# Attention in a hybrid encoder layer: the value product in two pieces instead of three, and the softmax sums added on GpSimd and VectorE

## The chip, the core and the metric

The kernel runs on one core of one Trainium2 chip. The metric is the device time of one execution in microseconds (us). The engines are TensorE (PE in the profile, PEld for its weight loads), VectorE (DVE), ScalarE (ACT), GpSimd (POOL) and the queue engine SyncE (SP).

## What is computed

One encoder layer over 2048 + 256 tokens of width 1024, in fp32: a joint input projection, eight mLSTM heads and eight attention heads side by side, an output projection with residual, and a convolutional feed-forward part. The change touches only the attention, whose reference is

```python
def block(qi):
    s = jnp.einsum('bqhgd,bkhd->bhgqk', qi, k).astype(jnp.float32) * scale
    p = jax.nn.softmax(s, axis=-1)
    return jnp.einsum('bhgqk,bkhd->bqhgd', p.astype(v.dtype), v)
```

with 64 columns a head, eight query heads on two key/value groups, and every query seeing all 2048 (or 256) keys of its sequence.

## The kernel before

To keep fp32 accuracy on TensorE, the kernel splits an operand in a rounded high part (type fp32r) and a low part, the rest, and multiplies high x high, high x low and low x high.

Attention (`attention`, lines 458 to 673) works on **head blocks**: 512 queries against all keys of their sequence. There are 36: four for the short sequence, with two key tiles of 128 keys, and 32 with sixteen. A block is walked in **steps** of two key tiles (eight steps, or one), 260 steps in all. One step is:

- `scores` (L577): four products of 512 columns (L583, L584) fill a score tile `ps` of two PSUM banks; ScalarE takes the exponential into `pe` (L587, 128 x 1024) and copies its high part into `x[:, 0]` (L588); VectorE subtracts for the low part `x[:, 1]` (L589).
- `values` (L592), some steps later: per key tile three products add into one PSUM bank `pv`. The stationary operand `vv` holds the high part of the values in columns 0 to 63 and ones in columns 64 to 127, so that rows 64 to 127 of `pv` gather the softmax sums; `vl` holds the low part of the values. L600 is `vv` x high weights, L601 `vl` x high weights, L602 `vv` x low weights.
- `maxstep` (L548): for the next block, two products (L560) and a maximum on VectorE (L562).

At a block's end `fin1` copies both halves of `pv` to SBUF with four ScalarE copies (L612); `fin2`, a step later, takes reciprocals of the sums (L617), multiplies (L618), and GpSimd's queue stores the result to `mix_d` (L624).

The score tiles, the maxima's tiles (`px`) and two small ones share a ring of two (tag "sc"); `pv` is one bank with one buffer. `PEB`, `XB` and `PLAG` are the buffers of `pe`, of `x`, and the number of steps by which `values` runs behind `scores`.

While attention runs, the other half of the program runs between its instructions: until about 1400 us the mLSTM heads (projection products L720, L730, L748; masks loaded by GpSimd's queue at L824 and cut by GpSimd at L828; GpSimd products `kw` at L793 and inverse roots at L97 and L98; VectorE work at L848 to L879), then the output projection (L1001). `run_both` (L1574) interleaves the two generators by weights; a scheduler then gives every engine its fixed order, which the engine follows instruction by instruction.

## Time and profile before

| what | before |
|---|---|
| time, median of 3 runs | 3317.97 us (3317.39 to 3322.92) |
| span of the profiled execution | 3315.5 us |
| busy: PE / weight loads / VectorE / ScalarE / GpSimd | 98% / 91% / 73% / 60% / 16% of the span |
| granted TensorE clock, mean | 0.992 |
| attention's steps | from 224 to about 1752 us |

The profile is of one execution, whose span (first to last instruction) is 3315.5 us. A group row gives line, engine, operation, output and inputs, shapes, count, then busy time and mean ns of one, then the idle time of the engine just before and what ended it. Rows of the timeline give start and length in us. Products overlap on PE, so that the length of one (about 0.40 us at 512 columns) is more than the distance between two.

### The profile page before, as it was taken

How to read it: one execution, taken by the hardware profiler on the slowest of the kernel's cores; microseconds unless marked ns; L12 is line 12 of the kernel's file. 1: busy time of each engine (PE TensorE's matmuls, PEld its weight loads, DVE VectorE, ACT ScalarE, POOL GpSimd, SP SyncE). 2: the span in 40 equal slices, each digit the busy share in tenths (PEclk: the TensorE clock that was granted, in tenths of full speed). 3: DMA queues.
4: the chain of work that ended last, by engine and by line, in shares of the span. 5: the costliest groups of instructions: out<-in, count | busy, mean ns of one | idle time of the engine just before them, and what ended most of it. 6: DMA issues, size and time to landing. Idle time of an engine off the chain costs nothing.

```text
span 3315.5 us, 53149 instructions
## 1 busy us (share of the span) xinstructions
PE 3240.5 (98%) x19488; PEld 3018.0 (91%) x19488; DVE 2429.5 (73%) x3759; ACT 1993.5 (60%) x3738; POOL 522.1 (16%) x917
## 2 busy tenths in 40 slices
PE   8989999999999999999999999999999999999998
PEld 7878888888888888788889999999999999999998
DVE  7755676676657768866666899998888889666654
ACT  5646666666675776655454555665676667454543
POOL 4561042223224323200000000000000000020101
PEclk9999999999999999999999999999999999999999
DMA  9973333343346444423227666767676567968663
GB/s 353 316 213 101 112 103 113 98 125 109 99 139 189 123 147 127 139 96 106 76 93 266 220 222 213 248 229 271 202 254 240 194 224 239 320 216 276 216 226 134
DMA packets 359117, 612.31 MB, mean 185 GB/s; under 512 B 31029, under 2 KB 215271, under 8 KB 358855
## 3 DMA queue, kind: packets, MB, share of 16 engines
q1 hardware_dynamic: 329431, 563.14, 50.5%
q0 software_dynamic: 11856, 33.96, 3.8%
q10 hardware_dynamic: 17568, 11.80, 1.1%
q8 instruction: 154, 2.52, 0.3%
q14 instruction: 108, 0.88, 0.1%
HBM read 444.85 MB, written 163.93 MB: 184 GB/s over the span
## 4 chain that ended last, share of the span: by engine, by line
PE 83%; issue 5%; DMA 4%; ACT 3%; DVE 3%; POOL 2%; SPq 1%; POOLq 0%; ACTq 0%; DVEq 0%
PE pa L1164 17%; PE pc L1164 8%; PE pf L1428 7%; PE po L1001 6%; PE pb L1164 4%; PE mj L720 4%; PE pj L238 4%; PE mv L730 4%; PE ph L1428 3%; PE ps L583 3%; PE pv L602 3%; PE pv L600 3%; PE ps L584 3%; PE pv L601 3%; PE px L560 3%
## 5 line engine op out<-in xcount | busy, mean ns | idle before, releaser
L589 DVE TENSOR_TENSOR xx<-pe,xx 128x1024 fp32r<-128x1024 f32 x260 | 319.0, 1227 | 171.4 <-ACT xx L588 169.9
L587 ACT ACTIVATE pe<-ps 128x1024 f32<-128x1024 f32 x260 | 266.1, 1024 | 231.8 <-PE ps L584 215.0
L562 DVE TENSOR_REDUCE mx<-px 128x1 f32<-128x1024 f32 x256 | 310.5, 1218 | 100.6 <-PE px L560 100.0
L588 ACT ACTIVATE xx<-pe 128x1024 fp32r<-128x1024 f32 x260 | 275.1, 1058 | 5.2 <-PE pv L602 0.2
L1381 POOL TENSOR_TENSOR sq<-sq,sq 128x384 f32<-128x384 f32 x38 | 48.5, 1277 | 1382.7 <-ACT sq L1377 1302.2
L1001 PEld LDWEIGHTS po<-cmx,wo 128*128 128x128 f32 x1728 | 229.9, 189 | 19.5 <-DVE cx L1008 1.1
L1001 PE MATMUL po<-cmx,wo 128*128 128x256 f32 x1728 | 238.7, 283 | 1.4 <-DVE cx L1008 1.0
L1168 ACT ACTIVATE u<-pa 128x386 f32<-128x386 f32 (+2 forms) x264 | 128.9, 489 | 173.9 <-PE pa L1164 168.7
L600 PE MATMUL pv<-xx,vv 128*128 128x512 f32 x520 | 212.4, 408 | 10.5 <-ACT rs L612 6.0
L583 PE MATMUL ps<-qq,kk 128*128 128x512 f32 x520 | 213.8, 411 | 8.2 <-ACT pe L587 3.9
L602 PE MATMUL pv<-xx,vv 128*128 128x512 f32 x520 | 211.0, 406 | 3.5 <-DVE xx L589 3.4
L584 PE MATMUL ps<-qm,kl 65*128 65x512 f32 x520 | 208.9, 402 | 0.0
L601 PE MATMUL pv<-xx,vl 128*64 128x512 f32 x520 | 207.3, 399 | 0.0
L720 PEld LDWEIGHTS mj<-mn,wm 128*128 128x128 f32 x1296 | 178.3, 193 | 18.3 <-ACT og L736 4.5
L720 PE MATMUL mj<-mn,wm 128*128 128x256 f32 x1296 | 189.6, 288 | 2.8 <-ACT og L736 2.8
L730 PE MATMUL mv<-wm,mn 128*128 128x256 f32 x1296 | 189.9, 286 | 1.3 <-ACT qb L726 1.3
L730 PEld LDWEIGHTS mv<-wm,mn 128*128 128x128 f32 x1296 | 176.1, 190 | 15.2 <-ACT qb L726 2.3
L238 PE MATMUL pj<-w_a,n1T 128*128 128x512 f32 (+1 forms) x864 | 167.8, 353 | 11.0 <-ACT w_a L105 7.1
L560 PE MATMUL px<-kk,qq 128*128 128x512 f32 x512 | 167.2, 408 | 2.4 <-ACT pe L587 2.4
L238 PEld LDWEIGHTS pj<-w_a,n1T 128*128 128x128 f32 x864 | 141.3, 192 | 30.6 <-ACT w_a L105 7.1
L1164 PE MATMUL pc<-nt,wb 128*128 128x386 f32 (+2 forms) x792 | 148.0, 341 | 0.0
L831 ACT ACTIVATE dm<-dm,tm 128x128 f32<-128x128 f32 x288 | 94.8, 392 | 86.0 <-POOL dm L828 85.7
(337 smaller groups left out, 8106.0 us busy)
## 6 DMA issues: line engine op xcount, KB each, us to landing
mn<-n_d SPq DMA_DIRECT2D x216, 256.0 KB, 3.1
ru<-w_up SPq DMA_DIRECT2D x88, 512.0 KB, 5.1
rs<-wsu_d SPq DMA_DIRECT2D x88, 512.0 KB, 5.7
act_d<-ts SPq DMA_DIRECT2D x33, 768.0 KB, 6.4
nt<-act_d SPq DMA_DIRECT2D x60, 384.0 KB, 5.2
re_t<-wsd_d SPq DMA_DIRECT2D x45, 512.0 KB, 5.4
wsu_d<-tw SPq DMA_DIRECT2D x44, 512.0 KB, 4.2
act_d<-ya SPq DMA_DIRECT2D x99, 192.0 KB, 2.1
```

Source lines behind the costliest of these rows:

```text
L238: nc.tensor.matmul(pjs[t][:, c0:c1], nTs[tiles[t]][:, c, a, :], ws[c][:, b, c0:c1], start=(c == 0 and k == 0), stop=(c == NCC - 1 and k == 2))
L562: nc.vector.tensor_reduce(s.mx[:, t0, z0:z0 + 1], ps, AX.X, ALU.max)
L583: nc.tensor.matmul(o, kk[:, kc:kc + P], s.qq, start=True, stop=False)
L584: nc.tensor.matmul(o, kl1[:, kc:kc + P], s.qm, start=False, stop=True)
L589: nc.vector.tensor_tensor(x[:, 1], pe, f32(x[:, 0]), ALU.subtract)
L600: nc.tensor.matmul(s.pv, vv[:, kt % 4, :], x1, start=kt == 0, stop=False)
L602: nc.tensor.matmul(s.pv, vv[:, kt % 4, :], x2, start=False, stop=kt == s.nk - 1)
L720: nc.tensor.matmul(pj[:, o].rearrange("p (n t) -> p n t", t=P), s.w[c][:, a, o * P:(o + 1) * P], nT[c][:, :, h, :], start=(c + o + k == 0) ...
L730: nc.tensor.matmul(pv[:, o], nT[c][:, o, a, :], s.w[c][:, h, 256:512], start=(c + o + k == 0), stop=(c == NCC - 1 and k == 2 and o == 1))
L1001: nc.tensor.matmul(po[:, o], wo[c][z // 2][:, a, n], mx[c][:, h, :], start=c + o + k == 0, stop=c == NCC - 1 and o == 1 and k == 2)
L1164: s.nc.tensor.matmul(p, w[:, aa, c, :], ops[k][:, c, bb, 0:s.n], start=c == 0 and i == 0 and not add, stop=c == NCC // 2 - 1 and i == 2, s ...
L1428: nc.tensor.matmul(ps[c], w[:, aa, c, :], t[:, gi - g0, bb, 0:H], start=gi == 0 and m == 0 and not more, stop=gi == NG - 1 and m == 2, ski ...
```

## The change

The value operand `vv` now holds the high part in columns 0 to 63 and the low part in columns 64 to 127, with no ones. Per key tile there are two products: `vv` x high weights (128 rows of `pv`: high and low part of the values) and the high part x low weights (64 rows). At a block's end the two halves of `pv` are added.

The sums are kept apart: from a block's second step on, the exponentials `pe` of the step before are added into this step's `pe`, columns 0 to 511 by GpSimd and 512 to 1023 by VectorE, once the subtraction has read it. After the last step GpSimd adds the two halves (`asum`), the sum is split in high and low part (`fin2`), two products with a tile of ones spread it over all rows (`fin3`), and reciprocal, multiplication and store follow (`fin4`). The three are taken one step after another. The buffers change: `pe` 3, `x` 3, lag 2.

```diff
-PEB = 2
-XB = 4
-PLAG = 3
+PEB = 3
+XB = 3
+PLAG = 2
...
-            vv = sp.tile([P, m, P], F32R, tag="vv" + s, name=f"vv{grp}_{s}", bufs=1)
-            vl = sp.tile([P, m, HD], F32R, tag="vl" + s, name=f"vl{grp}_{s}", bufs=1)
+            vv = sp.tile([P, m, 2, HD], F32R, tag="vv" + s, name=f"vv{grp}_{s}", bufs=1)
...
-            nc.gpsimd.memset(f32(vv[:, :, HD:P]), 1.0)
...
-            for a, t in ((0, vv[:, :, 0:HD]), (1, vl)):
-                nc.gpsimd.dma_start(f32(t), g.v_d[grp, :, k0 + t0:k0 + t0 + m, a])
+            nc.gpsimd.dma_start(f32(vv), g.v_d[grp, :, k0 + t0:k0 + t0 + m])
...
         nc.vector.tensor_tensor(x[:, 1], pe, f32(x[:, 0]), ALU.subtract)
+        if kp:
+            for z, eng in ((0, nc.gpsimd), (1, nc.vector)):
+                c = slice(512 * z, 512 * z + 512)
+                eng.tensor_tensor(pe[:, c], s.acc[:, c], pe[:, c], ALU.add)
+        s.acc = pe
+        if kp == s.nk // 2 - 1:
+            s.acc = sp.tile([P, 512], F32, tag="asum", name="asum" + s.nm, bufs=1)
+            nc.gpsimd.tensor_tensor(s.acc, pe[:, 0:512], pe[:, 512:1024], ALU.add)
...
-            nc.tensor.matmul(s.pv, vv[:, kt % 4, :], x1, start=kt == 0, stop=False)
-            nc.tensor.matmul(s.pv[0:HD], vl[:, kt % 4, :], x1, start=False, stop=False)
-            nc.tensor.matmul(s.pv, vv[:, kt % 4, :], x2, start=False, stop=kt == s.nk - 1)
+            for a in (0, 1) if z == 0 else (1, 0):
+                if a:
+                    nc.tensor.matmul(s.pv[0:HD], vv[:, kt % 4, 0], x2, start=False, stop=False)
+                else:
+                    nc.tensor.matmul(s.pv, vv[:, kt % 4].rearrange("p a d -> p (a d)"), x1, start=kt == 0,
+                                     stop=kt == s.nk - 1)
...
-            for r, o in ((0, s.o1), (HD, s.rs)):
-                nc.scalar.activation(o[HD * z:HD * z + HD], s.pv[r:r + HD, 256 * z:256 * z + 256], AF.Copy)
+            r, c = slice(HD * z, HD * z + HD), slice(256 * z, 256 * z + 256)
+            nc.scalar.activation(o2[r], s.pv[HD:P, c], AF.Copy)
+            nc.vector.tensor_tensor(s.o1[r], s.pv[0:HD, c], o2[r], ALU.add)
+
+    def fin2(s):
+
+        s.ah = sp.tile([P, 2, 512], F32R, tag="ah", name="ah" + s.nm, bufs=1)
+        nc.scalar.activation(s.ah[:, 0], s.acc, AF.Copy)
+        nc.vector.tensor_tensor(s.ah[:, 1], s.acc, f32(s.ah[:, 0]), ALU.subtract)
+
+    def fin3(s):
+
+        ps = pp.tile([P, 1024], F32, tag="sc", name="pa" + s.nm)
+        for a in range(2):
+            nc.tensor.matmul(ps[:, 0:512], g.onesr, s.ah[:, a], start=a == 0, stop=a == 1)
...
+            nc.scalar.activation(s.rs[r], ps[r, c], AF.Copy)
```

Since the scheduler sets the order, three places show what moved. In these rows a line number belongs to its own kernel (L600 to L602 before are L607 and L609 after, L589 is L586, L562 is L559, and L590 is the new addition); "waits" names the engine waited for; x3 counts equal rows.

TensorE before, in a block of head 4 while an mLSTM projection runs; `pv` is the value bank, `xx` the weights of a step, `ps` the scores:

```order
L602 MATMUL pv_4_5855<-xx_4_2_5825,vv_16_4_2556 128x512 [waits DVE_49]
L600 MATMUL pv_4_5855<-xx_4_2_5825,vv_16_4_2556 128x512
L601 MATMUL pv_4_5855<-xx_4_2_5825,vl_16_4_2557 64x512
L602 MATMUL pv_4_5855<-xx_4_2_5825,vv_16_4_2556 128x512
L583 MATMUL ps_4_4_6050<-qq_4_5303,kk_16_8_2570 128x512 [waits Activation_49]
L584 MATMUL ps_4_4_6050<-qm_4_5305,kl_16_8_2571 128x512
L583 MATMUL ps_4_4_6050<-qq_4_5303,kk_16_8_2570 128x512
L584 MATMUL ps_4_4_6050<-qm_4_5305,kl_16_8_2571 128x512
L600 MATMUL pv_4_5855<-xx_4_3_5851,vv_16_4_2556 128x512 [waits Activation_49]
L601 MATMUL pv_4_5855<-xx_4_3_5851,vl_16_4_2557 64x512
```

TensorE after, at the same step of the same block (`mj`, `mN`: mLSTM):

```order
L580 MATMUL ps_4_4_6108<-qq_4_5350,kk_16_8_2561 128x512 [waits DVE_49]
L581 MATMUL ps_4_4_6108<-qm_4_5352,kl_16_8_2562 128x512
L580 MATMUL ps_4_4_6108<-qq_4_5350,kk_16_8_2561 128x512
L581 MATMUL ps_4_4_6108<-qm_4_5352,kl_16_8_2562 128x512
L609 MATMUL pv_4_5891<-xx_4_3_5909,vv_16_4_2551 128x512 [waits Activation_49]
L745 MATMUL mj_6_7560<-mn_6_4_7548,wm_4_4882 128x256 [waits DMAHW7_49]
L745 MATMUL mj_6_7560<-mn_6_4_7548,wm_4_4882 128x256 x3
L888 MATMUL mN_16_7894<-va_8_2400,dm_16_7530 128x65 [waits DMASW7_49,PE_49,Activation_49]
L888 MATMUL mN_16_7894<-va_8_2400,dm_16_7530 128x65 x3
L607 MATMUL pv_4_5891<-xx_4_3_5909,vv_16_4_2551 64x512 [waits DVE_49]
L607 MATMUL pv_4_5891<-xx_4_3_5909,vv_16_4_2551 64x512
L609 MATMUL pv_4_5891<-xx_4_3_5909,vv_16_4_2551 128x512
```

The step's values are four products in place of six; those of the low weights (L607, the ones that wait for VectorE's subtraction) stand in the middle, with mLSTM products ahead of them.

VectorE before, a little earlier in the same block (`mx` is a maximum, `hh` and `s` belong to mLSTM):

```order
L562 TENSOR_REDUCE mx_4_5722<-px_4_0_1_5841 128x1 [waits PE_49]
L589 TENSOR_TENSOR xx_4_2_5825<-pe_4_2_5824,xx_4_2_5825 128x1024 [waits Activation_49]
L877 TENSOR_TENSOR hh_12_7041<-hh_12_7041,mr_12_7046 128x128 [waits DVE_49,Activation_49,Pool_49]
L879 SCALAR_TENSOR_TENSOR hh_12_7041<-ogr_12_6669,hh_12_7041 128x128 [waits DMASW3_49,DVE_49]
L562 TENSOR_REDUCE mx_4_5722<-px_4_1_1_5862 128x1 [waits PE_49]
L589 TENSOR_TENSOR xx_4_3_5851<-pe_4_3_5850,xx_4_3_5851 128x1024 [waits Activation_49]
L562 TENSOR_REDUCE mx_4_5722<-px_4_2_1_6066 128x1 [waits PE_49]
L589 TENSOR_TENSOR xx_4_4_6056<-pe_4_4_6055,xx_4_4_6056 128x1024 [waits Activation_49]
```

VectorE after, at the same steps; `pe` is the exponential, in which the sum is carried on, and `C` the mLSTM state:

```order
L559 TENSOR_REDUCE mx_4_5778<-px_4_0_1_5896 128x1 [waits PE_49]
L879 TENSOR_TENSOR s_16_7784<-mI_16_7781,tm 128x260 [waits PE_49]
L902 TENSOR_TENSOR hh_15_7767<-hh_15_7767,mr_15_7772 128x128 [waits DVE_49,Activation_49,Pool_49]
L586 TENSOR_TENSOR xx_4_2_5885<-pe_4_2_5884,xx_4_2_5885 128x1024 [waits Activation_49]
L904 SCALAR_TENSOR_TENSOR hh_15_7767<-ogr_14_7153,hh_15_7767 128x128 [waits DVE_49]
L559 TENSOR_REDUCE mx_4_5778<-px_4_1_1_5919 128x1 [waits PE_49]
L842 SCALAR_TENSOR_TENSOR C_9_4927<-C_8_4926,dec,C_9_4927 128x65 [waits Activation_49]
L590 TENSOR_TENSOR pe_4_2_5884<-pe_4_1_5854,pe_4_2_5884 128x512 [waits DVE_49]
L842 SCALAR_TENSOR_TENSOR C_10_4928<-C_9_4927,dec,C_10_4928 128x65 [waits DVE_49,Activation_49]
L586 TENSOR_TENSOR xx_4_3_5909<-pe_4_3_5908,xx_4_3_5909 128x1024 [waits Activation_49]
L590 TENSOR_TENSOR pe_4_3_5908<-pe_4_2_5884,pe_4_3_5908 128x512 [waits DVE_49]
```

Behind each subtraction (L586) stands an addition of half a tile (L590), once with a state update between, once right behind it; it waits for VectorE's own subtraction, and everything below it waits with it.

GpSimd before, in the same block (`dm` is a mask, `mr` an inverse root, `kw` an mLSTM product, `o` a block's result):

```order
L97 TENSOR_SCALAR mr_11_6914<-mms_11_6911 128x2 [waits Activation_49]
L98 TENSOR_TENSOR mr_11_6914<-mr_11_6914,mhalf 128x2 [waits Pool_49]
L836 DMA ogr_16_7457<-og_d 128x256 [waits DMAHW0_49,DMASW3_49,DVE_49]
L737 MEMSET va_4_4910 128x4
L793 TENSOR_TENSOR kw_6_6802<-mkt_3_6800,tm 128x256 [waits PE_49]
L793 TENSOR_TENSOR kw_7_6804<-mkt_3_6800,tm 128x256 [waits PE_49]
L624 DMA mix_d<-o_4_5835 64x256 [waits DVE_49,Activation_49]
L624 DMA mix_d<-o_4_5835 64x256 [waits DMASW5_49,Activation_49]
L824 DMA dm_15_7313<-nm_d 128x512 [waits DMASW6_49,PE_49]
L828 AFFINE_SELECT dm_15_7313<-dm_15_7313 128x256 [waits DMASW6_49]
L828 AFFINE_SELECT dm_15_7313<-dm_15_7313 128x256
```

GpSimd after, at the end of the block before and the start of this one; `asum` is the folded sum:

```order
L590 TENSOR_TENSOR pe_4_7_5754<-pe_4_6_5738,pe_4_7_5754 128x512 [waits DVE_49,Pool_49]
L594 TENSOR_TENSOR asum_4_5761<-pe_4_7_5754 128x512 [waits DVE_49,Pool_49]
L853 AFFINE_SELECT dm_17_7786<-dm_17_7786 128x256 [waits DMASW1_49]
L853 AFFINE_SELECT dm_17_7786<-dm_17_7786 128x256
L750 MEMSET qb_7_4958 64x2x128 [waits PE_49]
L750 MEMSET qb_7_4958 64x2x128 [waits Pool_49]
L97 TENSOR_SCALAR mr_14_7516<-mms_14_7513 128x2 [waits Activation_49,Pool_49]
L98 TENSOR_TENSOR mr_14_7516<-mr_14_7516,mhalf 128x2 [waits Pool_49]
L590 TENSOR_TENSOR pe_4_1_5854<-pe_4_0_5784,pe_4_1_5854 128x512 [waits DVE_49]
L849 DMA dm_0_8687<-nm_d 128x512 [waits PE_49]
L853 AFFINE_SELECT dm_0_8687<-dm_0_8687 128x256 [waits DMASW2_49]
```

The additions and the fold stand in one line with the masks' loads, cuts and inverse roots. An addition waits for VectorE (the subtraction that reads the same tile), and masks and roots wait behind it; the cut behind a load waits for that load, and the additions behind it.

More of the change, by code (lines that the diff above doesn't have):

```diff
@@ L493, in load_kv @@
             nc.gpsimd.memset(f32(kl1[64:65, :]), 1.0)
-            for a, t in ((0, vv[:, :, 0:HD]), (1, vl)):
-                nc.gpsimd.dma_start(f32(t), g.v_d[grp, :, k0 + t0:k0 + t0 + m, a])
-            parts.append((kk, kl1, vv, vl))
+            nc.gpsimd.dma_start(f32(vv), g.v_d[grp, :, k0 + t0:k0 + t0 + m])
+            parts.append((kk, kl1, vv))
     class HB:
@@ L643, in drain @@
             fin1(b)
-            fins.append(b)
+            fins.extend((f, b) for f in (fin2, fin3, fin4))
     for n in range(len(hbs)):
@@ L652, in attention @@
             pend.append((cur, *scores(cur, kp)))
-            ready = bool(fins)
+            ready = fins.pop(0) if fins else None
             if len(pend) > PLAG:
@@ L661, in attention @@
             if ready:
-                fin2(fins.pop(0))
+                ready[0](ready[1])
             yield 2.3
@@ L671, in attention @@
         yield 1
-    for b in fins:
-        fin2(b)
+    for f, b in fins:
+        f(b)
 def mlstm(g, tc, s1, sp, sw, sn, pj_, pm):
@@ L1522, in body @@
             sk = pool(s2, "b_k", bufs=1)
+            g.onesr = sk.tile([P, P], F32R, name="onesr")
+            nc.gpsimd.memset(f32(g.onesr), 1.0)
             sa = pool(s2, "b_s", bufs=2)
```

11 lines of the change are left out of this document (7 added, 4 removed).

## The prediction

> **What bounds the kernel now.** I read the head of the profile's page first, then the busy times of three stretches, then the groups of instructions, then the timeline. The page gives the span of the one profiled execution and the busy time of every engine; the stretches are from the first softmax step to the last mLSTM tile, from there to the last softmax step, and all that follows (columns: start and end, length, busy time and count of PE, PEld, DVE, ACT, POOL, granted clock, DMA share, GB/s).
>
> ```profile
> span 3315.5 us, 53149 instructions
> PE 3240.5 (98%) x19488; PEld 3018.0 (91%) x19488; DVE 2429.5 (73%) x3759; ACT 1993.5 (60%) x3738; POOL 522.1 (16%) x917
> ```
>
> ```profile
> 224.00:1400.00 1176.00, 1150.98 (x7264) 1001.94 (x7263) 807.82 (x1516) 767.48 (x1754) 331.48 (x652) 1.00 0.41 125
> 1400.00:1752.00 352.00, 344.88 (x2141) 298.69 (x2142) 235.51 (x329) 193.68 (x272) 14.69 (x23) 1.00 0.29 95
> 1752.00:3315.00 1563.00, 1538.27 (x8884) 1535.65 (x8882) 1221.22 (x1536) 908.38 (x1479) 58.64 (x50) 0.99 0.68 234
> ```
>
> The change touches only attention, so only the first two stretches, 1528 us together. PE is busy in 1495.9 of them (98%), VectorE in 1043.3 (68%), ScalarE in 961.2 (63%), GpSimd in 346.2. The groups say what a softmax step (one pair of key tiles) costs; there are 260 steps in 36 head blocks, 256 of them in 32 blocks of eight.
>
> ```profile
> L589 DVE TENSOR_TENSOR xx<-pe,xx 128x1024 fp32r<-128x1024 f32 x260 | 319.0, 1227 | 171.4 <-ACT xx L588 169.9
> L562 DVE TENSOR_REDUCE mx<-px 128x1 f32<-128x1024 f32 x256 | 310.5, 1218 | 100.6 <-PE px L560 100.0
> L588 ACT ACTIVATE xx<-pe 128x1024 fp32r<-128x1024 f32 x260 | 275.1, 1058 | 5.2 <-PE pv L602 0.2
> L587 ACT ACTIVATE pe<-ps 128x1024 f32<-128x1024 f32 x260 | 266.1, 1024 | 231.8 <-PE ps L584 215.0 <-DVE xx L589 5.3 <-DVE mx L562 3.2
> L600 PE MATMUL pv<-xx,vv 128*128 128x512 f32 x520 | 212.4, 408 | 10.5 <-ACT rs L612 6.0 <-ACT xx L588 4.1
> L602 PE MATMUL pv<-xx,vv 128*128 128x512 f32 x520 | 211.0, 406 | 3.5 <-DVE xx L589 3.4
> L601 PE MATMUL pv<-xx,vl 128*64 128x512 f32 x520 | 207.3, 399 | 0.0
> ```
>
> VectorE waits for ScalarE (171.4 us), ScalarE for PE (231.8 us), PE for next to nobody: PE sets the pace. But 0.40 us is a product's own length, not its price, since products overlap. The timeline of PE gives the price.
>
> ```profile
> 1500.02 0.40 PE L602 MATMUL pv<-xx,vv 128*128 128x512 f32 x1
> 1500.26 0.39 PE L600 MATMUL pv<-xx,vv 128*128 128x512 f32 x1
> 1500.49 0.39 PE L601 MATMUL pv<-xx,vl 128*64 128x512 f32 x1
> 1500.72 0.39 PE L602 MATMUL pv<-xx,vv 128*128 128x512 f32 x1
> 1500.95 0.28 PE L1001 MATMUL po<-cmx,wo 128*128 128x256 f32 x1
> ```
>
> Four products start within 0.93 us: 0.2325 us each, and the one with a 64-column stationary operand costs no less.
>
> **The products taken away.** A key tile has two value products in place of three: 520 fewer. Each head block gets two products with ones: 72 more. Net 448 x 0.2325 = 104.2 us of PE, 0.40 us a step. If PE went on setting the pace, the span would fall by that. The Trainium skill ("Perfetto Trace Analysis", section "Identifying the Most-Contended Engine") says to judge TensorE by the busy share of its weight loads rather than of its matmuls. That share is 85% in the first stretch and 98% in the last, so by the rule the gain would be cut to about 0.87 of it, an estimate of 91 us. The trace speaks against it here: a 0.19 us load under a 0.2325 us product cannot show more than 82%, and the five rows above have no gap. I keep 104.2.
>
> **The additions.** The row sums now come from VectorE (columns 512 to 1023 of the weights) and GpSimd (0 to 511), in 224 of the 260 steps (not in a block's first). Each block also folds its halves on GpSimd, splits the sum on VectorE and ScalarE, and adds the two halves of its result on VectorE. The nearest rows of those shapes, then of GpSimd (lowest, median and highest ns):
>
> ```profile
> L1015 DVE TENSOR_TENSOR cacc<-cacc,csq 128x512 f32<-128x512 f32 x26 | 17.9, 688 | 9.4 <-ACT csq L1011 9.3
> L864 DVE TENSOR_TENSOR s<-mN,s 128x260 f32<-128x260 f32 x72 | 30.1, 419 | 15.5 <-PE mN L863 15.3
> L612 ACT ACTIVATE rs<-pv 64x256 f32<-64x256 f32 x72 | 27.3, 380 | 1.6
> L539 ACT ACTIVATE qq<-pq 128x512 fp32r<-128x512 f32 x36 | 21.4, 594 | 5.5 <-PE pq L536 5.2
> ```
>
> ```profile
> L793 POOL TENSOR_TENSOR kw<-mkt,tm x72: 605/617/1682, 236.5 to 1220.7; 128x256 f32<-128x256 f32 x72
> L1381 POOL TENSOR_TENSOR sq<-sq,sq x38: 992/1133/1881, 2845.3 to 3281.9; 128x384 f32<-128x384 f32 x38
> L589 DVE TENSOR_TENSOR xx<-pe,xx x260: 1160/1224/1570, 224.0 to 1751.5; 128x1024 fp32r<-128x1024 f32 x130
> ```
>
> VectorE: 224 x 0.688 = 154.1, 36 x 0.688 = 24.8, 72 x 0.419 = 30.2, together 209.1 us or 0.804 us a step. ScalarE: 144 copies of 0.38 go; 144 of 0.38 and 36 of 0.594 come: +21 us on an engine with 37% to spare, which costs nothing as long as the exponential isn't late. GpSimd: from 256 to 384 columns the undisturbed time rises by 0.387 us, and by proportion from 384 it is 1.32 us; I take 1.35 us for 512 columns, between 1.32 and 1.38. 260 of them are 351 us: GpSimd doubles from 346 to 697 us. Fewer loads and fills of key and value tiles are a few us of GpSimd, off the path.
>
> Costed at nothing: the value products follow two steps behind the scores instead of three, with three weight tiles instead of four. Two steps are some 11 us, and the chain of exponential, copy and subtraction is 1.02 + 1.06 + 1.23 = 3.3 us, so 7 us of queueing are covered; beyond that each late subtraction stops PE. The sums' products take one turn more of the two score banks in each block, held for 2 x 0.2325 and two copies of 0.38, 1.2 us; the projection products of mLSTM and of phase C hide it, and it would cost 36 x 1.2 = 44 us if they didn't.
>
> **Who shares what.** The highest times above are no accident: a subtraction of 1.57 us and a kw of 1.68 us each overlapped the other engine.
>
> ```profile
> 304.88 1.23 DVE L589 TENSOR_TENSOR xx<-pe,xx 128x1024 fp32r<-128x1024 f32 x1 [2.66 <-ACT xx L588]
> 480.46 1.57 DVE L589 TENSOR_TENSOR xx<-pe,xx 128x1024 fp32r<-128x1024 f32 x1 [0.78 <-ACT xx L588]
> ```
>
> ```profile
> 304.90 1.68 POOL L793 TENSOR_TENSOR kw<-mkt,tm 128x256 f32<-128x256 f32 x1 [18.13 <-PE mu L806]
> 480.33 0.62 POOL L793 TENSOR_TENSOR kw<-mkt,tm 128x256 f32<-128x256 f32 x1 [1.46 <-PE mu L806]
> ```
>
> At 304.9 kw began 0.02 us behind the subtraction and took 1.06 us longer than its median: it waited it out. At 480.3 kw was first, and the subtraction took 0.35 us longer. So a VectorE operation with two inputs from SBUF and a GpSimd operation exclude one another, nearly from end to end. A GpSimd addition can therefore hold VectorE up by anything from 0 to 1.1 us (1.35 less the 0.25 that these pairs leave open). Both halves become ready when the subtraction ends. In 57 of 224 cases VectorE's half stands right behind the subtraction and goes first; else one to four others stand between, mostly reductions from PSUM or one-input work that need not wait. I take b = 0.4 us of delay a step, about a third of the 1.1.
>
> **The sum.** VectorE isn't evenly loaded. The busy times of the densest windows, then the subtractions in the same windows (which count steps), and a later window for what VectorE can reach:
>
> ```profile
> 400.00:500.00 100.00, 98.11 (x617) 85.32 (x617) 80.81 (x167) 69.38 (x164) 35.98 (x70) 1.00 0.34 102
> 700.00:800.00 100.00, 99.58 (x646) 88.37 (x645) 77.56 (x173) 66.59 (x163) 35.90 (x75) 1.00 0.39 116
> 1100.00:1400.00 300.00, 290.85 (x1741) 245.98 (x1742) 234.92 (x481) 205.39 (x477) 86.79 (x163) 0.99 0.42 129
> 2000.00:2100.00 100.00, 100.00 (x568) 99.96 (x567) 95.04 (x121) 59.61 (x93) 0.00 (x0) 1.00 0.59 207
> ```
>
> ```profile
> 400.00:500.00 100.00, 21.11 (x17) 1.00 0.34 102
> 700.00:800.00 100.00, 19.52 (x16) 1.00 0.39 116
> 1100.00:1400.00 300.00, 64.97 (x53) 0.99 0.42 129
> ```
>
> Dense part: 500 us, 86 steps, VectorE 393.3. It becomes 393.3 + 86 x (0.804 + 0.4) = 496.8; at the 95% that the window at 2000 shows, this needs 523.0 us: **+23.0**, since PE (500 - 86 x 0.40) no longer binds. The other 1028 us, 174 steps: VectorE 650.0 + 174 x 1.204 = 859.5, or 904.8 at 95%; PE 1028 - 69.8 = 958.2 still binds: **-69.8**. Handing over the one pv bank at a block's end: before, four copies of 0.38 on ScalarE, 1.51 us; now copy and addition twice, 2 x (0.376 + 0.419) = 1.59 us, and each block's first addition stands in VectorE's queue behind what is running, half of 1.22 us at 68% = 0.41. 36 x 0.5 = **+18.0**; the next block's first value product waits for it, and the scores behind that in PE's queue. Sum -28.8: span 3286.7. The median of the runs lies 2.5 us above the profiled span, so 3289 us.
>
> At b = 0 the dense part needs 486.8 and the sum is -65.0 (3253); at b = 1.1 both parts are VectorE's and it is +109 (3427). Zero lies at b = 0.70.
>
> **The rivals.** *PE keeps the pace everywhere:* VectorE's 32% of idle time takes the additions in, as its waits for ScalarE suggest (elastic, 170 us). Against it: 81% busy before anything is added. 104.2 less gives 3214; with the hand-over, 3232.
>
> *GpSimd's additions hold VectorE up for most of their length:* the place is the subtraction and the addition behind it in the mLSTM windows; VectorE becomes the bound of both parts; the point is b = 0.70. For it: each step has one GpSimd addition made ready by VectorE's own subtraction, so they meet every time, not by accident as kw does. At b = 0.9: dense 568.2 (+68.2), rest 996.3 (-31.7), +18: +54.6, 3373. The Trainium skill ("SBUF — State Buffer", section "SBUF: two separate sides") calls this pair of ports an exclusive lock for the whole instruction; the trace agrees but for some 0.25 us, and by the rule alone b could go to 1.35.
>
> *GpSimd's queue becomes the wait:* three pe tiles mean that an exponential needs the GpSimd addition two steps earlier, which stands in line behind mask work that waits for its load and behind stores that wait for a block's result.
>
> ```profile
> L624 POOL DMA_DIRECT2D mix_d<-o x70 | 38.6, 554 | 355.8 <-ACT xx L588 171.0 <-issue 71.1 <-ACT csq L1011 35.2
> ```
>
> ```profile
> POOL dm L828 <- DMA dm<-nm_d: 188.7, 66, 5.1
> ```
>
> The stores' 355.8 us fell when GpSimd had nothing else to do; in the new order additions stand behind them. The cover is two steps of some 5.5 us less 1.02 + 1.06 + 1.23 + 1.35, 6.3 us, against 5.1 us for the longest wait for a mask. If a third of 72 such waits of 2.86 us came through: +69, 3358.
>
> **Chances.** 3318 +- 6.6 (0.2%, what a measurement of this kernel can tell) counts as the same. PE keeps the pace, 3214 to 3250: 0.15. Forecast, 3250 to 3311: 0.45. Gain and loss even (b about 0.7): 0.10. Ports, 3325 to 3427: 0.22. GpSimd's queue: 0.08. Faster 0.60, same 0.10, slower 0.30. The range 3228 to 3370 leaves out the last part of the first rival (0.07) and of the ports (0.11).
>
> **What would show it.** Right: 1040 value products and 72 with ones; the stretch from first to last subtraction near 1500 us; VectorE at 88 to 95% in it (dense windows highest), PE there below 95%, idle ahead of value products put down to VectorE; subtractions and additions with maxima near 2.3 us; means of VectorE's additions near 1.0, of GpSimd's near 1.7 us. The port rival would show means of VectorE's additions near 1.5 us. GpSimd's queue would show exponentials waiting for GpSimd. I am wrong if PE stays above 97% there (first rival), or if the exponential's waits grow beyond 100 us with GpSimd as their releaser.

## The result, and the profile after

| | before | after |
|---|---|---|
| time, median of 4 runs each | 3317.68 us (3316.84 to 3322.92) | 3444.88 us (3442.93 to 3446.34) |
| span of the profiled execution | 3315.5 us | 3441.2 us |
| attention's stretch, from 224 us to its last step | 1528 us | 1662 us |
| what follows | 1563 us | 1555 us |

The ratio is 1.0387, 95% interval [1.0371, 1.0403]: slower by 127 us, where 29 us less were forecast, and above the range. Attention's stretch is 134 us longer, what follows 8 us shorter. The head of the page, then busy times of the mLSTM part, of the rest of attention's stretch, and of what follows, all of the kernel after:

```profile
span 3441.2 us, 53059 instructions
PE 3253.5 (95%) x19040; PEld 2992.1 (87%) x19040; DVE 2742.5 (80%) x4091; ACT 2022.2 (59%) x3774; POOL 906.6 (26%) x1154
```

```profile
224.00:1400.00 1176.00, 1080.80 (x6701) 931.09 (x6702) 968.08 (x1679) 737.70 (x1718) 580.43 (x798) 0.96 0.41 125
1400.00:1886.00 486.00, 437.33 (x2331) 354.11 (x2330) 389.51 (x501) 256.13 (x349) 150.13 (x116) 0.89 0.22 70
1886.00:3441.00 1555.00, 1528.62 (x8814) 1525.34 (x8812) 1221.42 (x1537) 905.33 (x1477) 61.64 (x52) 0.99 0.68 234
```

In 1662 us PE is busy for 1518.1 (91%, 98% before) and VectorE for 1357.6 (82%, 68% before). No engine is full. The groups, in attention's stretch:

```profile
L586 DVE TENSOR_TENSOR xx<-pe,xx 128x1024 fp32r<-128x1024 f32 x260 | 334.4, 1287 | 105.6 <-ACT xx L585 105.3
L559 DVE TENSOR_REDUCE mx<-px 128x1 f32<-128x1024 f32 x256 | 309.8, 1213 | 43.0 <-PE px L557 42.1
L584 ACT ACTIVATE pe<-ps 128x1024 f32<-128x1024 f32 x259 | 265.3, 1025 | 199.4 <-PE ps L581 127.8 <-DVE pe L590 31.5 <-POOL pe L590 17.5
L590 POOL TENSOR_TENSOR pe<-pe,pe 128x512 f32<-128x512 f32 x224 | 329.7, 1472 | 518.2 <-DVE xx L586 491.6 <-DVE m L565 13.6 <-DVE dn L893 4.4
L590 DVE TENSOR_TENSOR pe<-pe,pe 128x512 f32<-128x512 f32 x224 | 200.8, 896 | 4.0
L637 ACT ACTIVATE rs<-pa 64x256 f32<-64x256 f32 x70 | 26.4, 377 | 27.7 <-PE pa L633 27.1
L620 ACT ACTIVATE o<-pv 64x256 f32<-64x256 f32 x70 | 26.6, 380 | 35.7 <-PE pv L609 20.6 <-DVE o L621 14.0
```

The exponential (L584) used to wait for PE 215 us and for all else 17; it now waits for PE 128 us and for the two additions 49 us. In the same ScalarE line the copies of the sums (L637) wait 27 us for PE, and the copies of `pv` (L620) wait 14 us for VectorE's addition of the two halves. What TensorE waits for (waiting product, releaser, us, times, longest):

```profile
PE pv L607 <- DVE xx L586: 22.9, 22, 2.8
PE ps L580 <- DVE mx L559: 17.6, 18, 2.8
PE px L557 <- ACT pe L584: 16.9, 17, 2.7
PE pr L570 <- DVE m4r L567: 11.4, 9, 2.6
PE px L557 <- DVE mx L559: 9.7, 17, 1.5
```

In the kernel before none of these five was over 3.4 us. Waits have grown at several places where PE takes something from VectorE or ScalarE, not at one.

### The profile page after: what moved, and what is told of

It is laid out like the page before. It is cut to its first block, busy times and chain, and to the rows that moved or that the text cites. A ratio compares the mean times of both kernels' runs of the same rounds, so it can differ in the third digit from the quotient of the medians.

```text
span 3441.2 us, 53059 instructions
## 1 busy us (share of the span) xinstructions
PE 3253.5 (95%) x19040; PEld 2992.1 (87%) x19040; DVE 2742.5 (80%) x4091; ACT 2022.2 (59%) x3774; POOL 906.6 (26%) x1154
## 4 chain that ended last, share of the span: by engine, by line
PE 50%; DVE 8%; DMA 3%; issue 2%; ACT 2%; POOL 1%; SPq 0%; DVEq 0%; POOLq 0%; ACTq 0%
PE pa L1189 16%; PE pc L1189 8%; PE po L1026 6%; PE pf L1453 5%; PE pb L1189 4%; PE ph L1453 3%; PE pg L1453 2%; DVE xx L586 2%; DVE mx L559 2%; PE ps L580 1%; PE ps L581 1%; PE pv L607 1%; PE pv L609 1%; DMA nt<-act_d 1%; DVE pe L590 1%
## 5 line engine op out<-in xcount | busy, mean ns | idle before, releaser
L590 POOL TENSOR_TENSOR pe<-pe,pe 128x512 f32<-128x512 f32 x224 | 329.7, 1472 | 518.2 <-DVE xx L586 491.6
L586 DVE TENSOR_TENSOR xx<-pe,xx 128x1024 fp32r<-128x1024 f32 x260 | 334.4, 1287 | 105.6 <-ACT xx L585 105.3
L584 ACT ACTIVATE pe<-ps 128x1024 f32<-128x1024 f32 x260 | 266.3, 1025 | 199.7 <-PE ps L581 128.1
L559 DVE TENSOR_REDUCE mx<-px 128x1 f32<-128x1024 f32 x256 | 309.8, 1213 | 43.0 <-PE px L557 42.1
L580 PE MATMUL ps<-qq,kk 128*128 128x512 f32 x520 | 231.7, 445 | 24.5 <-DVE mx L559 17.6
L581 PE MATMUL ps<-qm,kl 65*128 65x512 f32 x520 | 222.1, 427 | 0.0
L609 PE MATMUL pv<-xx,vv 128*128 128x512 f32 x520 | 212.4, 427 | 6.7 <-ACT xx L585 6.1
L557 PE MATMUL px<-kk,qq 128*128 128x512 f32 x512 | 180.9, 436 | 27.0 <-ACT pe L584 16.9
L590 DVE TENSOR_TENSOR pe<-pe,pe 128x512 f32<-128x512 f32 x224 | 200.8, 896 | 4.0
L745 PEld LDWEIGHTS mj<-mn,wm 128*128 128x128 f32 x1296 | 176.5, 194 | 27.1 <-ACT og L761 12.0
L607 PE MATMUL pv<-xx,vv 128*64 128x512 f32 x520 | 176.8, 420 | 23.1 <-DVE xx L586 22.9
L580 PEld LDWEIGHTS ps<-qq,kk 128*128 128x128 f32 x520 | 107.2, 206 | 58.2 <-DVE mx L559 25.5
```

The lines of the kernel that those rows point to most:

```text
L559: nc.vector.tensor_reduce(s.mx[:, t0, z0:z0 + 1], ps, AX.X, ALU.max)
L580: nc.tensor.matmul(o, kk[:, kc:kc + P], s.qq, start=True, stop=False)
L584: nc.scalar.activation(pe, ps, AF.Exp)
L586: nc.vector.tensor_tensor(x[:, 1], pe, f32(x[:, 0]), ALU.subtract)
L590: eng.tensor_tensor(pe[:, c], s.acc[:, c], pe[:, c], ALU.add)
L745: nc.tensor.matmul(pj[:, o].rearrange("p (n t) -> p n t", t=P), s.w[c][:, a, o * P:(o + 1) * P], nT[c][:, :, h, :], start=(c + o + k == 0) ...
```

## The experiments

Several of these kernels leave out additions, sums or the low part of the values; they are for timing alone. In each section the first number is the median; "before" stood at 3314.7 to 3318.1 us beside them. Stretch is attention's, from 224 us to its last step.

### Undoing parts

**No additions** (the 448 additions out):

```diff
-        if kp:
-            for z, eng in ((0, nc.gpsimd), (1, nc.vector)):
-                c = slice(512 * z, 512 * z + 512)
-                eng.tensor_tensor(pe[:, c], s.acc[:, c], pe[:, c], ALU.add)
...
-            nc.scalar.activation(s.rs[r], ps[r, c], AF.Copy)
+            nc.scalar.activation(s.rs[r], ps[r, c], AF.Copy, bias=1.0)
```

> The changed kernel without the 224 additions on each of GpSimd and VectorE; it leaves out the sums of all steps but a block's last, so its output isn't the layer's. The fold, the split, the products with ones, the buffers and the lag stay. Theory of VectorE's line (the additions stand ahead of the subtractions and maxima that PE waits for) and theory of the ports (GpSimd's additions hold VectorE up): both expect that all of the loss goes with the additions, 3215 to 3250 us, clock back above 0.985. Theory of the lag (two steps and three weight tiles are too few): still above 3300 us. Theory of the block's end (fold, split, hand-over of the pv bank): above 3280 us.

3312.57 us, ratio 0.9991 [0.9979, 1.0003]. The additions cost 132 us, and the rest of the change gains next to nothing. The theories of VectorE's line and of the ports had counted on PE's 104 us here; the time lies where those of the lag and of the blocks' ends put it. Attention's stretch of this kernel (one execution of 3303 us, 9 below the median):

```profile
224.00:1744.00 1520.00, 1434.24 (x8957) 1237.78 (x8957) 1103.17 (x1948) 985.22 (x2060) 383.15 (x691) 0.98 0.39 118
```

PE's busy time fell from 1495.9 to 1434.2 us, and most of that became gaps: 86 us of idle time, 32 before.

**Two products, nothing else** (in the kernel before):

```diff
-            nc.tensor.matmul(s.pv[0:HD], vl[:, kt % 4, :], x1, start=False, stop=False)
```

> The kernel before, with one of its three value products a key tile left out (the low part of the values times the high part of the weights, 520 products); nothing else is changed, and that part of the result is missing. It takes 520 x 0.2325 = 121 us from PE without a later lag, without block-end work and without additions. If PE sets the pace of attention's stretch, as the prediction's first step said, the time falls to 3190 to 3230 us, and what took the gain away in the kernel without additions was the shorter lag and the blocks' ends. If the stretch is paced by the chain of scores, exponential, copy, subtraction and maxima through two score tiles, with PE merely filled up by other work, it stays at 3295 to 3320 us and PE's busy share of the stretch falls from 98% to about 91%.

3249.66 us, 0.9800 [0.9786, 0.9815], between the two ranges: 67 of 121 us come through. Attention's stretch of this kernel, and its exponential:

```profile
224.00:1694.00 1470.00, 1411.72 (x8966) 1250.22 (x8965) 1041.96 (x1856) 965.91 (x2033) 347.28 (x673) 0.99 0.41 123
```

```profile
L587 ACT ACTIVATE pe<-ps 128x1024 f32<-128x1024 f32 x259 | 265.1, 1024 | 165.7 <-PE ps L584 155.1 <-DVE xx L589 4.3 <-DVE dn L865 3.5
```

The exponential waits for PE 155 us instead of 215, so PE still releases it, but PE itself is now idle for 58 us of the stretch (32 before).

**The lag.** In the kernel before, and in the one just shown:

```diff
-PEB = 2
-XB = 4
-PLAG = 3
+PEB = 3
+XB = 3
+PLAG = 2
```

> The kernel before with the changed kernel's buffers and lag alone (pe 3, x 3, lag 2). Theory of the lag: 3350 us or more, with PE waiting for subtractions. The other theories: within 15 us of the kernel before (3305 to 3330 us).

> The kernel before with two value products a key tile (the low part of the values left out, as in the run at 3249.7 us), and with the change's lag of two steps, three weight tiles and three pe tiles. From 3249.7 to the kernel after without its additions (3312.6) are 63 us; this run tells how much of it is the lag. If the shorter lag is what lets value products wait for the subtraction (32.6 us of such waits without additions, 12.3 at 3249.7), it goes to 3275 to 3300 us. If the blocks' ends are what costs, it stays at 3250 to 3268 us, since the lag cost only 13 us with three products.

3327.92 us (1.0047 [1.0031, 1.0063]) with three products, 3251.23 us (0.9802 [0.9787, 0.9817]) with two. It costs 13 us where PE is full and 2 where it isn't, and both times lie where the theories other than the lag's put them. So the lag did not eat the gain.

**The blocks' ends.** First without additions and without all of the block's end (the copies into `rs` go as well, and `o1` has one buffer), then with the additions put back, with a lag of two steps and of three:

```diff
-            s.acc = sp.tile([P, 512], F32, tag="asum", name="asum" + s.nm, bufs=1)
-            nc.gpsimd.tensor_tensor(s.acc, pe[:, 0:512], pe[:, 512:1024], ALU.add)
...
-        nc.scalar.activation(s.ah[:, 0], s.acc, AF.Copy)
-        nc.vector.tensor_tensor(s.ah[:, 1], s.acc, f32(s.ah[:, 0]), ALU.subtract)
...
-            nc.tensor.matmul(ps[:, 0:512], g.onesr, s.ah[:, a], start=a == 0, stop=a == 1)
...
-            nc.vector.reciprocal(s.rs[:, c], s.rs[:, c])
-        nc.vector.tensor_tensor(s.o1, s.o1, s.rs, ALU.mult)
```

> The kernel after without additions and without the sums at a block's end (no fold, no split, no products with ones, no reciprocal and multiplication: the result isn't divided by the sums). Against the run without additions (3312.6) only the blocks' ends differ. If they are what costs, 3260 to 3280 us; if the lag is, 3290 to 3305 us, since 72 products (17 us) go in any case.

> The kernel after with its additions and its lag, without the sums at a block's end (the result isn't divided by them). If the blocks' ends cost much, 3380 to 3400 us (45 to 65 below the 3444.9 of the kernel after); if they cost little, 3420 to 3440 us.

> The kernel after with its 448 additions, without the sums at a block's end (the result isn't divided by them), and with the lag of three steps and four weight tiles of the kernel before. To be read against the same kernel with the lag of two steps, which runs beside it. If the additions cost what they do because they make the weights late for the value products, the third step of lag takes 40 us or more of it away. If they cost it because they make the scores' tiles free later (the maxima, which stand behind them in VectorE's line, and the exponentials, which wait for a pe tile), the lag helps by less than 20 us, about what it was worth in the kernel before.

3240.79 (0.9776 [0.9757, 0.9796]), 3343.56 (1.0072 [1.0051, 1.0094]) and 3330.80 us (1.0043 [1.0028, 1.0058]). A third step of lag is worth 13 us under the additions, as in the kernel before: they don't cost mainly by making the weights late for the value products. The first two lie below both of their expectations: 72 and 101 us for the blocks' ends. That is not the change's work alone, since the reciprocals had gone as well. So they were put back, with `rs` copied from the block's result as ones (the first cut is against the run without additions; fold, split and products with ones stay out), and taken from the kernel before (the second):

```diff
-            nc.scalar.activation(s.rs[r], ps[r, c], AF.Copy, bias=1.0)
+            nc.scalar.activation(s.rs[HD * z:HD * z + HD], s.o1[HD * z:HD * z + HD], AF.Copy, bias=1.0, scale=0.0)
```

```diff
-        for t in range(2):
-            c = slice(t * P, (t + 1) * P)
-            nc.vector.reciprocal(s.rs[:, c], s.rs[:, c])
-        nc.vector.tensor_tensor(s.o1, s.o1, s.rs, ALU.mult)
```

> The kernel after without additions and without fold, split and products with ones at a block's end, but with the copies of rs (from the block's result, as ones) and with the reciprocals and the multiplication, which the kernel before has as well (so the result isn't divided by the sums). The run without them all stood at 3240.8 us, the one with them all at 3312.6; the reciprocals of 0.94 us are 68 us of VectorE and were left out with the rest. If the 72 us are the change's own block ends, 3240 to 3265 us; if they were the reciprocals, 3290 to 3312 us.

> The kernel before without the reciprocals and the multiplication at a block's end (the result isn't divided by the sums): 82 us of VectorE's work in attention, 72 of them at 0.94 us and 36 at 0.41. If VectorE's work at a block's end sets the pace as it stands, already in the kernel before, 3250 to 3290 us; if PE sets it there, 3308 to 3318 us.

3268.62 (0.9859 [0.9843, 0.9876]) and 3306.57 us (0.9974 [0.9964, 0.9983]). The first is 4 us above the expectation for the change's own blocks' ends, the second 1 us below that for PE. The change's own sums there thus cost 3312.6 - 3268.6 = 44 us. Then the kernel without additions with the sums made, but their copies not waiting for PE:

```diff
-            nc.scalar.activation(s.rs[r], ps[r, c], AF.Copy, bias=1.0)
+            nc.scalar.activation(s.rs[r], s.o1[r], AF.Copy, bias=1.0, scale=0.0)
```

> The kernel after without additions (3312.6), with fold, split and products with ones, but the copies behind them on ScalarE read the block's result in place of the products' score tile, so that ScalarE doesn't wait for PE (16 to 27 us of such waits) and the score tile is free as soon as PE is done (the result isn't divided by the sums). If the third user of the two score tiles and ScalarE's wait are what costs, 3255 to 3280 us; if it is the work itself (VectorE's and GpSimd's in front, PE's 17 us), 3295 to 3312 us.

3294.77 us (0.9938 [0.9924, 0.9953]). ScalarE's copies of the sums, with them and (second) without the wait:

```profile
L633 ACT ACTIVATE rs<-pa 64x256 f32<-64x256 f32 x72 | 27.2, 377 | 18.3 <-PE pa L629 17.3
```

```profile
L633 ACT ACTIVATE rs<-o 64x256 f32<-64x256 f32 x72 | 29.9, 416 | 3.6 <-DVE o L617 1.8
```

The wait of 17.3 us is gone, and 17.8 us of time with it. The edit also lets go of the score tile as soon as PE is done with it, so the 17.8 us belong to the wait and the tile together. The time is at the edge of what the theory of the work itself gave, 15 us above the other: the larger half is work. Of these other 26 us the 72 products would be 16.7 (72 x 0.2325, an estimate at full price), and fold and split what remains (9); the two were not taken apart.

**One step later** (in the kernel after):

```diff
-            fins.extend((f, b) for f in (fin2, fin3, fin4))
+            fins.extend((f, b) for f in (lambda _: None, fin2, fin3, fin4))
```

> The kernel after, all of it, with the block's end (split, products with ones, multiplication) issued one step later, so that ScalarE's copy has one step more for GpSimd's fold to be done (16.9 us of waits). If waits in ScalarE's line are the cost of the block's end, 3410 to 3432 us; if not, 3438 to 3452 us.

3427.17 us (1.0336 [1.0320, 1.0351]), 18 us less, as expected, but not for the reason given: ScalarE's wait for the fold stays (16.9, now 19.3 us), and the one for the products with ones falls from 27.1 to 16.4.

### Which engine adds

One half alone, VectorE's or (second) GpSimd's, with one added to each sum as in the run without additions:

```diff
-            for z, eng in ((0, nc.gpsimd), (1, nc.vector)):
+            for z, eng in ((1, nc.vector),):
```

```diff
-            for z, eng in ((0, nc.gpsimd), (1, nc.vector)):
+            for z, eng in ((0, nc.gpsimd),):
```

> The kernel after with VectorE's half of the additions alone; GpSimd's 224 additions are left out, so half of the key columns are missing in the sums (one is added to each sum so that its reciprocal stays finite). From the kernel without additions (3312.6) to the kernel after (3444.9) it is 132 us. If what costs is the length that VectorE's own line gains (224 x 0.69 = 154 us of work ahead of the next maxima and subtractions), this run keeps about half to two thirds of it: 3375 to 3400 us. If what costs is the port between VectorE and GpSimd, this run has almost none of it: 3320 to 3340 us.

> The kernel after with GpSimd's half of the additions alone; VectorE's 224 additions are left out, so the other half of the key columns is missing in the sums (one is added to each sum). If VectorE's line is what costs, GpSimd's additions only cost through the instructions of VectorE that they hold up, and the run stays at 3325 to 3350 us. If the port is what costs, nearly all of the 132 us is here: 3400 to 3440 us, with subtractions well above their 1.22 us.

3362.25 us (1.0134 [1.0115, 1.0153]) with VectorE's half alone, 3359.53 us (1.0133 [1.0115, 1.0151]) with GpSimd's alone: 50 and 47 us above the run without additions. Neither theory: the halves cost alike, and both together 132, more than their sum. VectorE's busy time does the same: 1103.2 us of the stretch without additions, 1237.5 with VectorE's half, 1184.2 with GpSimd's and 1357.6 with both, 39 us more than the two increases (134.3 and 81.0) give together. The two halves hold each other up: VectorE's addition takes 0.695 us alone and 0.896 beside GpSimd's, GpSimd's 1.325 alone and 1.472 beside VectorE's. Then both halves and the fold on VectorE:

```diff
-            for z, eng in ((0, nc.gpsimd), (1, nc.vector)):
+            for z, eng in ((0, nc.vector), (1, nc.vector)):
...
-            nc.gpsimd.tensor_tensor(s.acc, pe[:, 0:512], pe[:, 512:1024], ALU.add)
+            nc.vector.tensor_tensor(s.acc, pe[:, 0:512], pe[:, 512:1024], ALU.add)
```

> The changed kernel with both halves and the fold on VectorE, none on GpSimd: VectorE gets 260 operations of 0.69 us more (about 179 us) and loses what GpSimd made it wait. Theory of the ports: faster than the changed kernel, 3380 to 3430 us, and VectorE's additions at 0.69 us each with no long ones. Theory of VectorE's line: slower than it, 3480 to 3600 us, since the work in the line grows. GpSimd's queue: faster, with no exponential waiting for GpSimd.

3439.89 us (1.0381 [1.0353, 1.0409]), the same as with GpSimd. All three theories miss: that of the ports alone (at most 3430) by 10 us, that of VectorE's line (at least 3480) by 40, and GpSimd's queue, which had expected less time. VectorE's rows of this kernel, then two of them in the kernel after:

```profile
L586 DVE TENSOR_TENSOR xx<-pe,xx 128x1024 fp32r<-128x1024 f32 x260 | 319.2, 1228 | 95.3 <-ACT xx L585 94.5
L590 DVE TENSOR_TENSOR pe<-pe,pe 128x512 f32<-128x512 f32 x448 | 294.0, 696 | 1.3
L842 DVE SCALAR_TENSOR_TENSOR C<-C,dec,C 128x65 f32<-128x65 f32 x128 | 38.6, 305 | 14.6 <-ACT C L834 13.5
L902 DVE TENSOR_TENSOR hh<-hh,mr 128x128 f32<-128x128 f32 x72 | 21.9, 305 | 33.5 <-POOL mr L98 33.3
```

```profile
L842 DVE SCALAR_TENSOR_TENSOR C<-C,dec,C 128x65 f32<-128x65 f32 x128 | 53.0, 417 | 10.9 <-ACT C L834 9.7
L902 DVE TENSOR_TENSOR hh<-hh,mr 128x128 f32<-128x128 f32 x72 | 33.6, 467 | 37.3 <-POOL mr L98 37.3
```

Without GpSimd's additions the subtraction is back at 1.228 us (1.287 with them) and an addition at 0.696 (0.896). So GpSimd holds VectorE up by (260 x 0.059 + 224 x 0.200) / 224 = 0.27 us a step in these two groups. VectorE's mLSTM work is held up as well (0.417 against 0.305 us for the state, 0.467 against 0.305 for `hh`): over all of VectorE's rows in the stretch, the same instructions take 136 us longer with GpSimd's additions than without, 0.61 us for each of the 224. Doing that half itself costs VectorE 224 x 0.696 and 36 folds of 0.695, 181 us. The delay is thus three quarters of the work that it spares, and VectorE's busy time is about the same (1373 against 1358 us of the stretch), which fits the equal times.

### What bounds the two kernels

An idle product a key tile (520, 121 us of PE; its stationary operand is zero) in the kernel after and in the one before, and 82 us of VectorE's work at the blocks' ends taken from the kernel after:

```diff
+            nc.tensor.matmul(s.pv[0:HD], g.zeror, x2, start=False, stop=False)
```

```diff
+            nc.tensor.matmul(s.pv[0:HD], g.zeror, x1, start=False, stop=False)
```

```diff
-            nc.vector.reciprocal(s.rs[:, c], s.rs[:, c])
-        nc.vector.tensor_tensor(s.o1, s.o1, s.rs, ALU.mult)
```

> The changed kernel with a third value product a key tile put back, of low weights with a stationary operand of zeros: 520 products of 512 columns, 121 us of PE, that change nothing in the result. Theory that PE still sets the pace: 121 us slower, 3560 us. Theory that VectorE's line sets it: the filler falls in PE's waits and costs less than 50 us, 3445 to 3495 us. Theory of the clock (PE's idle time lets the granted clock fall to 0.94 in the attention stretch, and this is what costs): granted clock in the stretch back above 0.97 and a time of at most 3445 us.

> The kernel before with one more product a key tile, with a stationary operand of zeros that adds nothing to the result: 520 x 0.2325 = 121 us of PE. In the kernel after the same work cost nothing (3434.2 against 3444.9). If PE set the pace before the change, the time rises by 85 to 125 us, to 3400 to 3440 us. If PE was only filled up with other work, as in the kernel after, it stays at 3310 to 3340 us.

> The kernel after without the reciprocals and the multiplication at a block's end (the result isn't divided by the sums): the same 82 us of VectorE's work, which the change does not touch, that were worth 10 us in the kernel before and 28 us in the one with two products and no sums. If VectorE's line has become what sets the time of attention's stretch, they are worth 50 to 85 us here: 3360 to 3395 us. If the stretch is bound by something else (GpSimd's additions, ScalarE's waits at a block's end), 15 us or less: 3430 to 3445 us.

3434.20 (1.0370 [1.0350, 1.0390]), 3408.86 (1.0276 [1.0261, 1.0292]) and 3399.74 us (1.0250 [1.0233, 1.0267]). The idle product costs 91 us before, as expected where PE sets the pace. After, the time is 11 us less with it: below the range for VectorE's line, and within what the theory of the clock had asked for (taken up in the last section). The VectorE work is worth 45 us after, 10 before, and at most 28 with two products and no sums (3268.6 against 3240.8, where 72 copies into `rs` on ScalarE go as well). Attention's stretch of the three, in this order:

```profile
224.00:1872.00 1648.00, 1559.01 (x9524) 1313.94 (x9523) 1349.17 (x2174) 992.34 (x2062) 737.90 (x913) 0.98 0.36 109
```

```profile
224.00:1819.00 1595.00, 1574.83 (x9680) 1342.47 (x9679) 1039.17 (x1820) 960.54 (x2013) 336.19 (x674) 1.00 0.37 110
```

```profile
224.00:1843.00 1619.00, 1494.67 (x9104) 1280.14 (x9104) 1288.52 (x2081) 991.43 (x2068) 739.95 (x915) 0.95 0.37 112
```

The last lies 5 us above its range for VectorE's line and 30 below the other. In the kernel before the idle product leaves PE at 99% of a longer stretch; in the kernel after it fills PE's gaps (91 to 95%), VectorE stays at 82%, and nothing gets longer.

**Spreading mLSTM** over more of attention, in the kernel after:

```diff
-LEAD = 1.3
+LEAD = 1.1
```

> The kernel after with one number changed: the lead that mLSTM's instructions are given over attention's, 1.3 to 1.1. In the kernel after, mLSTM ends at 1390 us while attention has about 88 of its 260 steps to go, and output-projection work runs out in parts of what follows (0, 6 and 52 products in three windows of 50 us, granted clock 0.75 to 0.80). If that lack of other work is part of the cost, spreading mLSTM further brings 20 to 60 us back: 3385 to 3425 us. If attention's chain alone sets the time, it stays at 3435 to 3455 us.

3462.24 us (1.0442 [1.0424, 1.0459]), above both ranges: attention ends at 1850 instead of 1886, but what follows takes 52 us more, 1607 instead of 1555. The lack of other work isn't cured that way.

### The ladder

Each row adds one part to the one above; shares of attention's stretch are worked out from its busy times in the one profiled execution.

| kernel | us | step | stretch | PE | VectorE |
|---|---|---|---|---|---|
| before (beside the two products) | 3316.8 | | 1528 | 98% | 68% |
| two products (low part of the values out) | 3249.7 | -67 | 1470 | 96% | 71% |
| lag 2 | 3251.2 | +2 | 1473 | 96% | 71% |
| new hand-over of `pv`, low part back in | 3268.6 | +17 | 1482 | 96% | 72% |
| fold, split, products with ones | 3312.6 | +44 | 1520 | 94% | 73% |
| additions: after | 3444.9 | +132 | 1662 | 91% | 82% |

## Why the prediction was wrong

**PE sets the pace before: right, but not at full price.** 121 us more of PE cost 91 (0.75 of it), 121 us less brought 67 (0.55). The row of the groups by which the exponential waits 215 us for PE was read rightly. What was read wrongly is the busy share of 98% as having no slack. The Trainium skill's rule ("Perfetto Trace Analysis", section "Identifying the Most-Contended Engine"), to judge TensorE's headroom by the busy share of its weight loads, would have cut the gain to 0.87 by the prediction's estimate, the right way but milder than the measured 0.55. The trace doesn't bear out the share as a measure of the slack here: with the idle product added, PE is 99% busy and the loads' share is 84%, against 85% before.

**The hand-over of `pv`: right in size, by luck.** +18.0 forecast, +17 measured (the step also reorders two products and moves the copies of `rs`). The wait that the prediction named, PE's next value product for the bank, is not there: 4.1 us in the run with two products and lag 2, 0.9 in the run with the new hand-over. What is new there is ScalarE's wait for VectorE's first addition of the halves, 14 us, which the prediction doesn't have; that it makes the 17 us is not shown.

**Costed at nothing.** The lag: +2 to +13 us. The sums' use of a score tile was to be hidden by projection products and cost 44 us if it weren't. It is not hidden: ScalarE, not PE, stands in its line until the products are done, with the exponentials behind it. That wait and the tile cost 17.8 us, less than the bound. With the products' PE time (16.7 us, which the sum had) and what remains for fold and split (9), the sums cost 44; that this equals the bound is chance.

**The lengths: right. The ports: under-sized, and not what failed.** VectorE's additions have a mean of 0.896 us (forecast near 1.0), GpSimd's 1.472 (near 1.7), and the longest subtraction and addition take 2.4 and 2.7 us (near 2.3). By the forecast, 260 steps of 1.204 us bring VectorE to 1043.3 + 313.0 = 1356.3 us busy or blocked; it shows 1357.6. The match is partly luck. The lengths of all of VectorE's instructions in the stretch grow by 346 us: 210 of work, as forecast (209.1), and the 136 of delay, 0.52 us for each of 260 steps where b = 0.4 was taken. But records of neighbouring instructions overlap a little, so that the busy time grows less than the lengths. At b = 0.52 the prediction's own sum would still have come out 18 us faster (an estimate by its formula). The two pairs of rows from which b was bounded leave 0.15 us open (1.23 - 0.02 - 1.06, and 0.62 - 0.13 - 0.35), not 0.25, which moves the bound from 1.1 to 1.2 and nothing else.

The rival of the ports gave a time that is nearer (3325 to 3427), but by a b above 0.70 that is not there, and the run with all additions on VectorE has no such delay and the same time. GpSimd's queue as a wait: 17.5 us of exponentials, not 69. The measured time lies above every time that was given a chance.

**The step that failed is the sum.** It let VectorE reach 95% of the dense part, let PE go on binding the other 1028 us, and so put the additions at +57 us (23.0 where PE alone would have given -34.4, and nothing elsewhere). They cost 132. VectorE, busy as forecast, reached 82% of the stretch, and not 95% even in the same dense windows, where steps had become fewer: 70 in 500 us, 7.1 us each, where the forecast had 86 in 523, 6.1 each. Nor did PE go on binding the rest: there 190 steps took 1162 us, 6.1 us each, against 5.9 before and 5.5 forecast (the windows are the same times, not quite the same steps). Busy times of the kernel after, then its subtractions there (17, 16 and 53 before):

```profile
400.00:500.00 100.00, 94.83 (x617) 82.28 (x616) 91.04 (x178) 64.00 (x154) 55.63 (x88) 1.00 0.40 119
700.00:800.00 100.00, 98.00 (x657) 87.34 (x656) 90.43 (x180) 68.53 (x174) 62.71 (x98) 1.00 0.39 119
1100.00:1400.00 300.00, 264.39 (x1473) 217.84 (x1474) 263.04 (x498) 184.16 (x434) 135.11 (x188) 0.90 0.40 122
```

```profile
400.00:500.00 100.00, 19.83 (x15) 1.00 0.40 119
700.00:800.00 100.00, 18.52 (x14) 1.00 0.39 119
1100.00:1400.00 300.00, 51.10 (x41) 0.90 0.40 122
```

The 95% had come from a stretch behind attention, where VectorE serves a PE that is never waiting. In attention PE, ScalarE and VectorE hand each step around: scores, exponential, copy, subtraction, value products, and the maxima beside them through the same two score tiles. The sum took the larger of two engines' times in each part; the runs show a passage between them. The same 82 us of VectorE are worth 10 us at a share of 68% of the stretch, at most 28 at 72% and 45 at 82%, and the same 121 us of PE are worth 91 us at 98% and no time at 91%, net of a clock that they brought back. That this is so because each engine keeps its fixed order, so that any late step leaves gaps on the next engine, fits the waits that grew at several links; which link decides was not separated. That both halves of the additions cost 35 us more together than one by one goes with the 39 us that VectorE is busy longer because they hold each other up.

Of the signs named: PE below 95% and VectorE as releaser of value products came; a stretch near 1500 us and VectorE at 88 to 95% of it did not.

## What to carry to other kernels

When work moves from an engine that is 98% busy to one that is 70% busy in the same loop, the new time isn't the larger of the two busy times: price both sides, by leaving the products out alone (here 0.55 of their length came through, 2.0% of the time, with the low part of the values missing) and by taking some work from the receiving engine. Look at a block's end for an engine that stands in its line until a small product comes back, since the step's critical instruction may be next in that line.

## What the hardware showed unasked

The granted clock of TensorE fell where PE had short gaps: 0.96 and 0.89 in the two parts of the stretch after, where both were 1.00 before. It is not the main cause: in the windows from 400 and from 700 us, shown above, the clock is 1.00, and 15 and 14 steps stand where 17 and 16 stood. What it adds in the later part was not separated: with the idle products the stretch's clock is back at 0.98 (0.94 without) and the time 11 us less, but these products are 121 us of PE's work themselves, so the clock alone may be worth more than 11 us.

A reciprocal of 128 x 128 takes VectorE longer than an addition of four times as many columns. Its group in the kernel after:

```profile
L642 DVE RECIPROCAL rs<-rs 128x128 f32<-128x128 f32 x72 | 63.4, 918 | 4.9 <-ACT rs L637 4.8
```

That is 7.2 ns a column, against 0.696 us / 512 = 1.4 ns for the undisturbed addition.
